# Later transposes of the expert lists in a two-layer decoder step

## The chip, the cores and the metric

The kernel runs on one core of a Trainium2 chip. The time is the device time of one execution in microseconds (us). Five engines work beside each other, each with a queue of its own that it takes strictly in order: TensorE (PE, and PEld for its weight loads), VectorE (DVE), ScalarE (ACT), GpSimd (POOL) and SyncE (SP, which only issues transfers here).

## The reference, cut to what matters

One inference step of a two-layer trunk (an RWKV-7 mixer, then a Mamba-2 mixer, each followed by an expert channel mixer called PEER) for a prompt of 256 tokens with 16 meta tokens, and for 32 sample tokens. The change lies in PEER, which runs once in each layer:

```python
q = (xt @ w_q).reshape(T, P_HEADS, 2, P_QDIM // 2)        # 8 heads, two half queries
s = jnp.einsum('thzd,zhkd->thzk', q, sub_keys)            # 128 scores a half
sv, si = lax.top_k(s, P_TOPK)                             # 16 best of each half
cand = sv[:, :, 0, :, None] + sv[:, :, 1, None, :]        # their 256 sums
top_s, pos = lax.top_k(cand..., P_TOPK)                   # 16 best of these: experts
gate = jax.nn.softmax(top_s, axis=-1)
act = jax.nn.gelu(jnp.einsum('td,ted->te', x_blk, u_tab[i_blk]))
out = jnp.einsum('te,ted->td', gate * act, v_tab[i_blk])  # 128 of 16384 experts a token
```

## The kernel before, in words

PEER (`peer`, line 838) does not gather the experts of the prompt tokens. It multiplies all 256 prompt tokens with the whole u table, in 128 blocks of 128 experts, takes GELU, multiplies the result by a sparse matrix of gates (zero for experts that a token has not chosen), and multiplies that with the whole v table in 128 blocks. Only the 48 sample and meta tokens (tile 0 of the selection) gather their expert rows by indirect transfers.

A **u product** (`s_chunk`, line 1060) is one such block: SP fetches 512 KB of weights (`wraw`, three buffers); ACT casts them to `whi` (line 276); POOL subtracts to get the low part `wlo` (line 281; `leng=LP` with LP = 8 gives POOL the whole of it in this stage); PE runs 16 matmuls with `whi` (lines 302 and 303) and 8 with `wlo` (line 305); ACT applies GELU from PSUM into `G` (line 1065). `whi` and `wlo` have two buffers each. The first 56 u products (b = 0 to 55, B0 = 56) run beside the selection.

The **expert selection** (`topk`, line 926 on) is nearly all DVE work: maxima, indices, candidate sums and a chain of comparisons (lines 957 to 1002) for three tiles: tile 0 (the sample and meta tokens, 64 rows), tiles 1 and 2 (two prompt tiles of 128 tokens). It is written as a generator of which the product loop takes a step or two a product, so its DVE work is interleaved with the products. They lie in a part of `G` that the one-hot stage fills later. Each tile ends with three lists on which the rest depends: `af` (line 1002) and `bf` (line 1001), the two halves of the expert numbers, and `ts`, the gates. For the gates three pieces are called later, from a table:

- `exps` (line 1004): ACT's exponential, which needs a table load before and another one behind it;
- `gates` (lines 1007 to 1009): DVE's sum, reciprocal and product, which give `ts`;
- `finish` (lines 1011 to 1017) for the prompt tiles: three PE transposes of `af`, `bf` and `ts` into one PSUM tile `ptk` (line 1014) and one ACT copy of it into `sel` (line 1017). For tile 0 the third piece is `indices` (lines 1019 on), which writes expert numbers through DRAM with POOL's transfers.

The table is `AFTER` (line 1075): row ti gives the u products behind which the three pieces of tile ti are called. Inside a PEER block a planner orders the instructions of each engine by its own estimate of time, but the first instruction of `exps` and `gates`, the first transpose and the copy are tied with `keep_in_program_order`: they stay behind everything of their engine that is written ahead of them.

Behind product 55 comes the **one-hot stage** (lines 1089 to 1124): for each group of four tokens DVE, ACT and POOL build two one-hot matrices from `sel` (`onehots`; three buffers, so three groups can be ready ahead), PE multiplies them (`pwt`, line 1120), DVE multiplies the result into `G` (line 1121) and ACT copies the rest (line 1122); ten more u products are mixed in. Tile 1's half of `sel` serves the first 32 groups, tile 2's half the last 32. Then come the v products (`acc`, line 1273) to the end of PEER.

Of the kernel before, what the change touches and what calls it, by code (L numbers as in the profile page):

```python
# [225 lines left out]
class K:  # L226
# [611 lines left out]
    def peer(self, l, ng):  # L838
# [233 lines left out]

        tk = chain(topk(0), topk(1), topk(2))

        AFTER = ((14, 16, 55), (29, 31, 39), (46, 46, 52))
        for b in range(B0):
            s_chunk(b, G[:, b], leng=LP if b < LB else None, tag="so"[b % 2])
            next(tk, None)
# [2 lines left out]
            for ti in range(3):  # L1081
                for i in range(3):
                    if b == AFTER[ti][i]:
                        late[ti][i]()
# [615 lines left out]
```

## Time and profile before

| | us |
|---|---|
| median of 3 runs (2675.41 to 2686.91) | 2676.23 |
| the profiled execution | 2676.22 |
| its span, first to last instruction | 2674.4 |

| engine | busy us | share of the span |
|---|---|---|
| PE | 2506.7 | 94% |
| PEld | 2156.3 | 81% |
| DVE | 1912.9 | 72% |
| ACT | 1246.7 | 47% |
| POOL | 1012.7 | 38% |

The profiled execution is 1.8 us longer than its span. PE is busy nearly all the time, so the question for each of its idle stretches is what ended it. Times in the rows count from the start of the span. The 56 products beside the selection stand near 500 to 690 us in the first layer and near 1820 to 2008 us in the second.

### The profile page before, as it was taken

The page shows a single profiled execution, that of the slowest core. Times are in us where ns is not written, and L with a number is a line of the kernel's source. Part 1 is how long each engine was busy: PE and PEld are TensorE (multiplying, and loading weights), DVE is VectorE, ACT ScalarE, POOL GpSimd, SP SyncE. Part 2 cuts the span into 40 slices and gives each one's busy share as a digit, 9 for nine tenths or more (in the row PEclk, how much of TensorE's full clock was granted, in tenths as well). Part 3 has the DMA queues.
Part 4 walks back from the last instruction along what each step waited for, and adds up shares of the span by engine and source line. Part 5 has one row for each costly group of instructions (what it writes and reads, how often), then busy time and mean ns, then how long its engine had stood idle before and what let it go on. Part 6 is the DMA issues. An engine that isn't in the chain of part 4 may idle for free. (4 is left out here: it accounts for less than half of the span.)

```text
span 2674.4 us, 47364 instructions
## 1 busy us (share of the span) xinstructions
PE 2506.7 (94%) x18281; PEld 2156.3 (81%) x18281; DVE 1912.9 (72%) x3713; ACT 1246.7 (47%) x2324; POOL 1012.7 (38%) x895
## 2 busy tenths in 40 slices
PE   7999999996989999999978888999979899999998
PEld 4677769996978888888765776899979788888886
DVE  5355556897695777788784787769949856776777
ACT  3322233453784444444454543335448744444444
POOL 4111110485980233424146455106959501122220
PEclk9999999998999999999999999999989999999999
DMA  3111115453417788888732443454633267788784
GB/s 148 52 46 44 41 58 174 138 179 105 136 42 213 255 304 303 299 301 311 256 93 87 146 154 124 129 181 148 184 110 114 62 217 250 259 279 260 262 270 156
DMA packets 125858, 460.68 MB, mean 172 GB/s; under 512 B 14816, under 2 KB 15744, under 8 KB 122432
## 3 DMA queue, kind: packets, MB, share of 16 engines
q1 hardware_dynamic: 99488, 361.08, 42.0%
q0 software_dynamic: 26144, 96.56, 10.1%
q8 instruction: 144, 2.36, 0.4%
q14 instruction: 82, 0.67, 0.1%
HBM read 440.90 MB, written 16.69 MB: 171 GB/s over the span
## 5 line engine op out<-in xcount | busy, mean ns | idle before, releaser
L276 ACT CAST whi<-wraw 128x1024 fp32r<-128x1024 f32 (+1 forms) x619 | 641.9, 1038 | 892.0 <-PE acc L1273 283.5
L283 DVE TENSOR_TENSOR wlo<-wraw,whi 128x1024 fp32r<-128x1024 f32 (+1 forms) x493 | 601.2, 1220 | 423.8 <-ACT whi L276 326.9
L302 PE MATMUL psc<-xh,whi 128*128 128x256 f32 x2048 | 509.0, 285 | 4.6 <-ACT h L1065 2.6
L303 PE MATMUL psc<-xl,whi 128*128 128x256 f32 x2048 | 507.0, 284 | 0.0
L281 POOL TENSOR_TENSOR wlo<-wraw,whi 128x1024 fp32r<-128x1024 f32 (+1 forms) x150 | 357.5, 2390 | 181.3 <-PE pq L305 72.5
L302 PEld LDWEIGHTS psc<-xh,whi 128*128 128x128 f32 x2048 | 392.8, 192 | 12.0 <-ACT whi L276 3.0
L303 PEld LDWEIGHTS psc<-xl,whi 128*128 128x128 f32 x2048 | 392.9, 192 | 5.6
L305 PE MATMUL psc<-xh,wlo 128*128 128x256 f32 x2048 | 291.6, 284 | 0.3 <-POOL wlo L281 0.3
L1051 POOL DMA_INDIRECT G<-in_un,gi x80 | 112.1, 1401 | 472.6 <-DVE glo L283 308.9
L1273 PE MATMUL acc<-whi,glo 128*128 128x512 f32 x1024 | 284.4, 398 | 6.7 <-DVE glo L283 6.7
L1273 PE MATMUL acc<-whi,gh 128*128 128x512 f32 x1024 | 284.6, 398 | 4.4 <-ACT whi L276 3.3
L1273 PE MATMUL acc<-wlo,gh 128*128 128x512 f32 x1024 | 281.8, 396 | 0.0
L305 PEld LDWEIGHTS psc<-xh,wlo 128*128 128x128 f32 x2048 | 265.2, 192 | 1.2 <-POOL wlo L281 0.7
L1273 PEld LDWEIGHTS acc<-whi,glo 128*128 128x128 f32 x1024 | 193.3, 189 | 54.6 <-DVE glo L283 7.6
L1148 POOL DMA_INDIRECT G<-in_v,gi x80 | 120.1, 1502 | 302.7 <-DVE G L1143 165.7
L1273 PEld LDWEIGHTS acc<-wlo,gh 128*128 128x128 f32 x1024 | 192.7, 189 | 47.8 <-DVE wlo L283 1.3
L1273 PEld LDWEIGHTS acc<-whi,gh 128*128 128x128 f32 x1024 | 184.0, 189 | 44.8 <-ACT whi L276 6.5
L1120 PE MATMUL pwt<-ob,oa 128*128 128x128 f32 x1024 | 144.7, 281 | 11.6 <-DVE ob L1094 8.0
L1120 PEld LDWEIGHTS pwt<-ob,oa 128*128 128x128 f32 x1024 | 127.7, 191 | 23.1 <-issue 19.2
L302 PE MATMUL pi<-xh,whi 128*128 128x320 f32 x328 | 107.0, 337 | 13.1 <-ACT cst L1369 4.7
L303 PE MATMUL pi<-xl,whi 128*128 128x320 f32 x328 | 105.8, 334 | 4.1 <-DVE xl L336 3.8
L283 DVE TENSOR_TENSOR glo<-G,gh 128x256 fp32r<-128x256 f32 x256 | 106.7, 418 | 2.7 <-ACT gh L276 2.7
(485 smaller groups left out, 4462.4 us busy)
## 6 DMA issues: line engine op xcount, KB each, us to landing
wraw<-in_u SPq DMA_DIRECT2D x256, 512.0 KB
wraw<-in_v SPq DMA_DIRECT2D x256, 512.0 KB
wraw<-in_win SPq DMA_DIRECT2D x41, 512.0 KB
wraw<-in_wq SPq DMA_DIRECT2D x32, 512.0 KB
wraw<-in_rkv SPq DMA_DIRECT2D x24, 512.0 KB
h<-in_ssm SPq DMA_DIRECT2D x8, 1024.0 KB
out_sssm<-h POOLq DMA_DIRECT2D x8, 1024.0 KB, 4.7
wraw<-in_wo SPq DMA_DIRECT2D x8, 512.0 KB
```

The costliest lines, as they stand in the source:

```text
L276: self.nc.scalar.copy(hi, x)
L281: self.nc.gpsimd.tensor_sub(lo[:, :n], x[:, :n], hi[:, :n].bitcast(F32))
L283: self.nc.vector.tensor_sub(lo[:, n:], x[:, n:], hi[:, n:].bitcast(F32))
L302: nc.tensor.matmul(ps, lhsT=whi[:, k], rhs=xhi[:, x0 + k], start=start and k == 0, stop=False)
L303: nc.tensor.matmul(ps, lhsT=whi[:, k], rhs=xlo[:, x0 + k], start=False, stop=False)
L305: nc.tensor.matmul(ps, lhsT=wlo[:, k], rhs=xhi[:, x0 + k], start=False, stop=stop and k == kb - 1)
L1051: nc.gpsimd.indirect_dma_start(out=rows, out_offset=None, in_=a[f"un{l}"], in_offset=bass.IndirectOffsetOnAxis(ap=gi[:, 0, g, m:m + 1], ax ...
L1120: mm(pw[:, j], lhsT=oa[:, j], rhs=ob[:, j], start=True, stop=True)
L1148: nc.gpsimd.indirect_dma_start(out=rows, out_offset=None, in_=vrows, in_offset=bass.IndirectOffsetOnAxis(ap=gi[:, 1, g, m:m + 1], axis=0))
L1273: mm(acc[i], lhsT=g[:, t0:t0 + 128], rhs=w[:, d0:d0 + 512], start=b == 0 and g is gh and w is vhf, stop=b == 127 and w is vlf)
```

## The change

The first prompt tile's transposes are called behind product 52 instead of 39, the second prompt tile's behind product 55 (the last of the 56) instead of 52. The second tile's `exps` and `gates` are called one product sooner, behind 45. Tile 0's row and tile 1's `exps` and `gates` stay.

```diff
-        AFTER = ((14, 16, 55), (29, 31, 39), (46, 46, 52))
+        AFTER = ((14, 16, 55), (29, 31, 52), (45, 45, 55))
         for b in range(B0):
             s_chunk(b, G[:, b], leng=LP if b < LB else None, tag="so"[b % 2])
             next(tk, None)
             if b % 2:
                 next(tk, None)
             for ti in range(3):
                 for i in range(3):
                     if b == AFTER[ti][i]:
                         late[ti][i]()
```

## Rows read from the trace of the kernel before

**Rows 1.** PE's waits, whole span: waiter, releaser, total us, times, longest.
```profile
PE ptk L1014 <- DVE G L1009: 20.5, 2, 10.2
PE ptk L1014 <- DVE G L1001: 18.7, 2, 9.4
```
**Rows 2.** PE in time, layer 0: start, us, line, operation, [idle before <-releaser].
```profile
614.22 1.12 PE L305 MATMUL psc<-xh,wlo 128*128 128x256 f32 x8
...
640.44 0.47 PE L1014 MATMUL ptk<-c,G 128*128 128x128 f32 x1 [10.23 <-DVE G L1009]
...
681.40 0.49 PE L1014 MATMUL ptk<-c,G 128*128 128x128 f32 x3
```
**Rows 3.** The same of layer 1.
```profile
1933.71 1.12 PE L305 MATMUL psc<-xh,wlo 128*128 128x256 f32 x8
...
1958.36 0.47 PE L1014 MATMUL ptk<-c,G 128*128 128x128 f32 x1 [10.23 <-DVE G L1009]
```
**Rows 4.** Stretches: length, busy PE, PEld, DVE, ACT, POOL (instructions), PE clock, DMA share, GB/s.
```profile
640.90:643.00 2.10, 2.10 (x12) 2.10 (x11) 2.07 (x2) 2.02 (x7) 1.45 (x3) 0.50 0.03 8
...
860.00:1200.00 340.00, 336.96 (x1919) 292.10 (x1918) 256.49 (x349) 158.85 (x238) 105.44 (x73) 1.00 0.85 290
```
**Rows 5.** PE in time, layer 0, products 13 and 14.
```profile
537.79 1.12 PE L305 MATMUL psc<-xh,wlo 128*128 128x256 f32 x8
540.67 1.12 PE L305 MATMUL psc<-xh,wlo 128*128 128x256 f32 x8
```
**Rows 6.** POOL in time, layer 0, before and behind the gap.
```profile
612.70 2.41 POOL L281 TENSOR_TENSOR wlo<-wraw,whi 128x1024 fp32r<-128x1024 f32 x1 [0.47 <-ACT whi L276]
...
641.55 0.81 POOL L1105 TENSOR_SCALAR oa<-cp,sel 128x128 f32<-128x128 f32 x1 [23.63 <-ACT sel L1017]
```
**Rows 7.** DVE in time, layer 0, inside PE's gap.
```profile
619.56 0.28 DVE L1002 TENSOR_TENSOR G<-G 128x128 f32<-128x128 f32 x1
...
622.31 2.27 DVE L996 TENSOR_TENSOR G<-G,cp 128x2048 bf16<-128x2048 f32 x1
...
625.95 0.27 DVE L984 TENSOR_TENSOR G<-G 128x128 f32<-128x128 f32 x1
...
632.79 1.22 DVE L992 TENSOR_TENSOR G<-G 128x1920 bf16<-128x1920 bf16 x1
...
640.10 0.28 DVE L1009 TENSOR_TENSOR G<-G 128x128 f32<-128x128 f32 x1
640.30 1.22 DVE L1000 TENSOR_TENSOR G<-G 128x2048 bf16<-128x2048 bf16 x1
641.55 2.29 DVE L1001 TENSOR_REDUCE G<-G 128x128 f32<-128x2048 bf16 x1
```
**Rows 8.** DVE in time, layer 0, ahead of the gap, beside POOL's subtractions.
```profile
556.59 2.71 DVE L989 TENSOR_TENSOR G<-G,cp 128x448 bf16<-128x448 bf16 x1
559.23 2.90 DVE L992 TENSOR_TENSOR G<-G 128x960 bf16<-128x960 bf16 x1
...
567.47 1.80 DVE L984 TENSOR_TENSOR G<-G 128x128 f32<-128x128 f32 x1
569.46 0.21 DVE L993 TENSOR_TENSOR G<-G 128x64 f32<-128x64 f32 x1
569.59 2.43 DVE L1002 TENSOR_TENSOR G<-G 128x64 f32<-128x64 f32 x1
...
584.72 3.21 DVE L996 TENSOR_TENSOR G<-G,cp 128x1024 bf16<-128x1024 f32 x1
```
**Rows 9.** DVE in time, layer 0, behind the gap.
```profile
643.76 0.76 DVE L1094 TENSOR_TENSOR ob<-cp,sel 128x512 f32<-128x512 f32 x1
...
648.49 2.42 DVE L1105 TENSOR_SCALAR oa<-cp,sel 128x128 f32<-128x128 f32 x1
...
668.40 1.46 DVE L1009 TENSOR_TENSOR G<-G 128x128 f32<-128x128 f32 x1
```
**Rows 10.** ACT in time, layer 0: the GELU of product 39.
```profile
615.41 0.38 ACT L1065 ACTIVATE G<-psc 128x256 f32<-128x256 f32 x1
```

## The prediction, on record before the changed kernel ran

> **What bounds the kernel now.** I read the busy shares first: PE is busy 94% of the span, so an idle stretch of PE is time lost unless something later absorbs it. Next the list of PE's waits over the whole span [rows 1]. Its two longest entries, 20.5 and 18.7 us, are the same instructions: the transposes `ptk` of a selection list, waiting for DVE. They come twice, once in each layer, so I read PE in order of time around the first of them [rows 2]. Product 39's last matmuls end at 614.22 + 1.12 = 615.34, then only three transposes run until 640.44 + 0.47 = 640.91. In the second layer the gap goes from 1934.83 to 1958.83 [rows 3]. In these gaps the other engines' rows say who works: POOL waits 23.63 us behind its last subtraction [rows 6], and DVE runs the tail of the selection without a pause [rows 7]. So for some 50 us in all this kernel is bound by DVE's list work and not by PE. The second tile's transposes, behind product 52, show no wait: three run in 0.49 us [rows 2].
>
> After the gap the work is PE's again: in the 340 us from 860 on PE is busy 336.96 [rows 4], so time saved ahead of that arrives at the end; I see no transfer or list that would hold it at an absolute time.
>
> **The change part by part.** The sum is made against the profiled execution's own 2676.22 us (span 2674.4 and 1.8 around it), which is the median, 2676.23, too.
>
> *The wait behind product 39 goes.* The gap is 640.91 - 615.34 = 25.6 us in layer 0 and 24.0 in layer 1. The three transposes themselves stay, 0.5 us without waits, so 25.1 and 23.5 go. Behind the gap PE runs 2.1 us at a granted clock of 0.50, the lower of its two levels (1.2 of 2.4 GHz), after it was idle [rows 4]; at full clock this work takes half, so another 1.05 us a layer. Together 26.1 + 24.5 = 50.6 us. That is the most the change can give.
>
> *What is late next.* Products 40 to 52 now follow at once. The pace is 2.88 us (537.79 to 540.67, [rows 5]); beside the selection it was 614.22 - 540.67 = 73.55 us for the 25 products 15 to 39, 2.94 each, so 13 products take 38.2 us with 0.8 of it lost to the neighbours. PE then reaches the first tile's transposes at 615.3 + 38.2 = 653.5 in layer 0 and 1973.0 in layer 1. The gates `ts` were ready at 640.10 + 0.28 = 640.4 [rows 7] and 1958.3 (the transposition that waited for them starts at 1958.36, [rows 3]). On those dates PE would not wait at all.
>
> But those dates were reached while POOL stood still. With no gap POOL subtracts on, 2.41 us of every 2.88 [rows 6], and DVE's instructions beside it are far longer. Compare the same lines without and with POOL: L1002 took 0.28 us in the gap and 2.43 ahead of it, on half the elements; L996 2.27 against 3.21 on half the elements (some 1.15 alone); L992 1.22 against 2.90 on half; L984 0.27 against 1.80; L989 took 2.71, on half the elements too, and L993 only 0.21 [rows 7, 8]. Some are stretched by about 2 us and some, which fall between two subtractions, not at all. From 618 us to the gates DVE has fifteen instructions of these kinds (tensor-tensor, scalar-tensor-tensor and cast): L993 twice, L1002 twice, L994 twice, L996 twice, and one each of L984, L1000, L982, L987, L989, L992 and L1009. By the rows: L1002 2 x 2.2 = 4.4, L996 2 x 2.1 = 4.2, L984 1.5, L992 2.90 - 0.61 = 2.3, L989 like L992 2.3, L1009 like L1002 2.2, L982 like L984 1.5, and nothing for L993, as its row shows, nor for L994, L987 and L1000, of which I have no stretched row. That is 18.4 us. Bounds: 0 if all find a gap, and 15 x 2.41 = 36 if each waits a whole subtraction. I take 18.4, since it goes line by line.
>
> The Trainium skill, page "SBUF — State Buffer", section "SBUF: two separate sides", says that DVE and GpSimd share a port pair under an exclusive lock which whoever starts first holds for its whole instruction. The stretched rows agree; read strictly, it would put the cost nearer to 36 us than to 18.4, which is the third case below.
>
> So `ts` of tile 1 is ready at 640.4 + 18.4 = 658.8 and 1958.3 + 18.4 = 1976.7. PE, there at 653.5 and 1973.0, waits 5.3 and 3.7 us. For a wait that short I take half of the 1.05 us of lower clock, 0.5 (ends 0 and 1.05).
>
> *The copy and the one-hots behind it.* ACT's copy into `sel` and POOL's first one-hot stand in their queues as before, now behind product 52. ACT holds the casts of the next weights meanwhile, but two are ready, and PE waits for the same event. What is new is the cover. DVE, ACT and POOL made the first three groups of one-hots 40 us ahead of their use. DVE spent 643.76 to 650.9 on them, 7.2 us [rows 9]. Now DVE, from 658.8 on, has L1000 and L1001 of tile 2 (1.22 + 2.29, [rows 7]), tile 2's gates (1.46 for the last of them, about 1.9 in all, [rows 9]) and then the one-hots: 658.8 + 3.5 + 1.9 + 7.2 = 671.4. PE, from 659 on, has three products (8.6 us) and the second transposes and is ready for `pwt` at 668.4. The first group is ready by then, the third is not. I charge 2 us a layer, between 0 and 3.0 (671.4 - 668.4).
>
> *The second tile.* Its transposes move behind product 55. PE gets there near 668 us, and `ts` of tile 2 is done near 664: no wait, 4 us of margin. Its `exps` (a table load, 0.31 us and a load back, as before) come one product sooner on ACT. ACT is there at the GELU of product 45: 615.41 + 0.38 + 6 x 2.9 = 633.2 [rows 10]. The maxima are subtracted (L984) at 626.2 in the gap [rows 7], and with L1002, L996 and L984 stretched (2.2 + 2.1 + 1.5) at 632.0: cost nothing, with 1 us of margin. POOL's index transfers of tile 0 stay behind product 55, SP's queue holds the same transfers in the same order, and both come sooner with PE. ACT's later copy over the lists follows `pwt`, which PE issues behind the transposes.
>
> *Sum.* Layer 0: 26.1 - 0.8 - 5.3 - 0.5 - 2.0 = 17.5. Layer 1: 24.5 - 0.8 - 3.7 - 0.5 - 2.0 = 17.5. 2676.2 - 35.0 = **2641 us**. Its own range, with half of the contention (9 us, no wait, nothing for the clock: gains of 23.3 and 21.7) and with half as much again (28 us: waits of 15 and 13, gains near 8): 2631 to 2660.
>
> **The rivals.**
> *All of it comes out.* If DVE's tail meets few subtractions and the one-hots hide under the last products, only 0 to 0.8 us a layer are lost: 2676.2 - 50.6 = 2625.6, or 2627. For it: DVE has 13 us of slack to the new place. Against it: five of the six lines in [rows 8] were stretched.
> *The wait only moves.* If all fifteen wait a whole subtraction (the strict reading of the skill's page), `ts` comes at 676.4 and PE waits 22.9 and 21.3 us at product 52. 26.1 - 22.9 - 0.8 - 1 = 1.4 and as much in layer 1: 2673. Against it: as soon as PE waits, POOL runs out of weights after two of them and DVE is free again, so it is more like 2660 at worst.
> *Slower.* ACT, tied behind product 45, takes `exps` of tile 2 in strict order. Should DVE's order or its contention bring L984 of tile 2 late, ACT waits with the casts behind it, and PE starves when the two buffered weights are used. Each us later than 633 + 5 costs PE one. The change is a loss when that exceeds 17.5 us a layer, L984 later than about 655. If the planner put L984 behind tile 1's gates (658.8) it would cost 21 a layer: 2676.2 + 2 x 3.5 = 2683. Against it: in the order of before L984 stands 14 us ahead of these gates.
> *Not what it says.* If the planner's other orders shift with the ties, so that PE waits elsewhere for the same lists, the time stays near 2676.
>
> **How the numbers follow.** Forecast 0.58; all of it 0.22; the wait moves 0.10; slower 0.04; nothing changes 0.06. The range 2623 to 2660 leaves out the last two and most of the third. A measurement can tell 0.5%, 13.4 us: faster means below 2662.8. That holds for the first two cases and half of the third, 0.85; within 0.5%: the other half and nothing changes, 0.11; slower than 2689.6 only if L984 is later still, 0.04.
>
> **What would show it.** PE's gap behind product 39 is gone, and a shorter one of some 4 to 5 us for L1009 stands ahead of the first `ptk` at about 654 us. DVE's L1002, L996, L992 and L1009 of tiles 1 and 2 are as long as ahead of the gap now. `pwt` begins 15 to 19 us sooner in each layer, and everything behind it keeps its length. Wrong would be: a wait of PE for `whi` near product 46 (ACT held by `exps`), a wait at product 52 above 12 us, or an unchanged DVE tail with a total near 2626.

## The result and the profile after

The changed kernel takes 2647.46 us (median of 4 runs, 2643.12 to 2648.49) against 2675.82 for the kernel before in the same comparison (4 runs, 2674.05 to 2686.91). The ratio is 0.9879, with a 95% interval of 0.9862 to 0.9895: 1.2% faster. In two later comparisons, on other runs, the changed kernel took 2641.48 us (ratio 0.9863, 0.9843 to 0.9882) and 2643.80 us (0.9875, 0.9858 to 0.9891). The forecast was 2641 us, a gain of 35.0 us; in the three comparisons the median lies 28.4, 35.2 and 34.1 us below that of the kernel before beside it. The profiled execution took 2643.12 us, with a span of 2641.3.

PE's waits over the whole span (waiter, releaser, total us, times, longest). In the kernel before there was a third one at `ptk`, beside the two of [rows 1]:

```profile
PE ptk L1014 <- DVE G L1002: 7.6, 2, 4.6
```

Of the changed kernel:

```profile
PE ptk L1014 <- DVE G L1009: 7.3, 2, 4.7
...
PE psc L305 <- POOL wlo L281: 1.6, 5, 0.5
...
PE pwt L1120 <- DVE ob L1103: 1.5, 1, 1.5
```

The waits for L1001 and L1002 are no longer in the list, and the one for L1009 has shrunk from 20.5 to 7.3 us. 20.5 + 18.7 + 7.6 = 46.8 us of waits at `ptk` have become 7.3. The two lowest lines are small: POOL's low parts were waited for once and for 0.3 us in the kernel before, and the one-hot of L1103 not at all.

PE in order of time, first layer 0 and then layer 1 (start, us, line, operation, [idle before <-releaser]); these lines answer to [rows 2] and [rows 3]:

```profile
655.17 1.12 PE L305 MATMUL psc<-xh,wlo 128*128 128x256 f32 x8
656.13 0.38 PE L1014 MATMUL ptk<-c,G 128*128 128x128 f32 x2
659.10 0.33 PE L1014 MATMUL ptk<-c,G 128*128 128x128 f32 x1 [2.59 <-DVE G L1009]
...
670.11 1.57 PE L1120 MATMUL pwt<-ob,oa 128*128 128x128 f32 x10 [1.53 <-DVE ob L1103]
...
674.28 0.49 PE L1014 MATMUL ptk<-c,G 128*128 128x128 f32 x3
```
```profile
1958.49 1.12 PE L305 MATMUL psc<-xh,wlo 128*128 128x256 f32 x8
1959.45 0.38 PE L1014 MATMUL ptk<-c,G 128*128 128x128 f32 x2
1964.58 0.48 PE L1014 MATMUL ptk<-c,G 128*128 128x128 f32 x1 [4.75 <-DVE G L1009]
```

Behind product 52 (the L305 line ahead of each) two transposes go at once, and the third waits for the gates. The three transposes of tile 2 (674.28) still wait for nothing. Stretches of the changed kernel (length, busy PE, PEld, DVE, ACT, POOL, PE clock, DMA share, GB/s), for [rows 4]:

```profile
653.90:660.10 6.20, 3.61 (x30) 3.38 (x30) 6.20 (x6) 3.02 (x6) 5.44 (x3) 1.00 0.46 124
660.10:663.60 3.50, 3.50 (x19) 3.50 (x18) 3.46 (x2) 3.50 (x11) 3.50 (x3) 0.51 0.69 213
860.00:1200.00 340.00, 335.57 (x1910) 290.38 (x1909) 259.28 (x353) 158.00 (x236) 110.97 (x76) 1.00 0.85 291
```

PE is busy for 3.61 of the 6.20 us around the wait, and in the 3.50 us behind it the granted clock is 0.51, the lower of its two levels. In the v products PE is busy 335.57 of 340 us, nearly as before.

Now the engines that set the date of the gates. DVE in order of time in layer 0, from 618 us to the gates; the lines answer to [rows 7], and they now look like those of [rows 8]:

```profile
618.69 1.57 DVE L993 TENSOR_TENSOR G<-G 128x128 f32<-128x128 f32 x1
620.18 0.28 DVE L1002 TENSOR_TENSOR G<-G 128x128 f32<-128x128 f32 x1
...
623.98 4.05 DVE L996 TENSOR_TENSOR G<-G,cp 128x2048 bf16<-128x2048 f32 x1
...
629.39 1.05 DVE L984 TENSOR_TENSOR G<-G 128x128 f32<-128x128 f32 x1
630.37 3.43 DVE L1000 TENSOR_TENSOR G<-G 128x2048 bf16<-128x2048 bf16 x1
633.72 2.43 DVE L982 CAST G<-G 128x128 f32<-128x128 uint32 x1
636.06 2.27 DVE L1001 TENSOR_REDUCE G<-G 128x128 f32<-128x2048 bf16 x1
638.26 2.18 DVE L987 TENSOR_TENSOR G<-G,cp 128x1920 bf16<-128x1920 f32 x1
640.47 3.17 DVE L989 TENSOR_TENSOR G<-G,cp 128x896 bf16<-128x896 bf16 x1
643.57 3.42 DVE L992 TENSOR_TENSOR G<-G 128x1920 bf16<-128x1920 bf16 x1
...
656.61 2.43 DVE L1009 TENSOR_TENSOR G<-G 128x128 f32<-128x128 f32 x1
```

POOL's subtractions in the same time, one line each:

```profile
626.35 3.94 POOL L281 TENSOR_TENSOR wlo<-wraw,whi 128x1024 fp32r<-128x1024 f32 x1 [0.48 <-ACT whi L276]
...
630.26 2.45 POOL L281 TENSOR_TENSOR wlo<-wraw,whi 128x1024 fp32r<-128x1024 f32 x1
...
632.68 3.38 POOL L281 TENSOR_TENSOR wlo<-wraw,whi 128x1024 fp32r<-128x1024 f32 x1
...
636.02 2.40 POOL L281 TENSOR_TENSOR wlo<-wraw,whi 128x1024 fp32r<-128x1024 f32 x1
...
638.38 4.31 POOL L281 TENSOR_TENSOR wlo<-wraw,whi 128x1024 fp32r<-128x1024 f32 x1
```

Read the two lists together. L996 stretches to 628.03; POOL's subtraction that started at 626.35 ends 2.26 us behind that, at 630.29, nearly its usual 2.41. L984, issued at 629.39, ends at 630.44, just behind that subtraction. POOL's next runs to 632.71, and L1000 ends 1.09 us later, against 1.22 alone [rows 7]. The next subtraction ends at 636.06, 2.26 us behind L1000, and the cast L982 ends at 636.15. So at these places the two engines take turns, and each instruction waits for the rest of the other's. Beside the reduction L1001 neither waits: it takes 2.27 us and the subtraction 2.40. L987 takes 2.18, as long as it does alone, because it starts 0.12 us ahead of a subtraction; that one pays instead, with 4.31.

The Trainium skill, page "SBUF — State Buffer", section "SBUF: two separate sides", says that the shared port pair goes to whoever starts first for its whole instruction and that the other blocks; the trace agrees, within some 0.15 us at each turn. The same page, section "Who interferes with whom", says that `tensor_reduce` never contends on this chip; L1001 and L998 (2.14 us with and without POOL) agree.

To compare kernels without what happens elsewhere I take the **stage** of a layer: from the GELU of product 39 to the last line of `pwt` in the one-hot stage. Before: 796.10 - 615.41 = 180.7 us in layer 0 and 2113.80 - 1934.90 = 178.9 in layer 1. The table has its gain in each traced kernel (us), layer 0 / layer 1. It also has the sum of the durations of the fifteen DVE instructions of the prediction, which was 12.65 and 13.84 us in the two gaps of the kernel before (tile 1's gates come last among them, so kernels with another order have none). The last column has what PE waited for up to its first one-hot product and with it, where a wait was 1 us or longer:

| kernel | stage gain | DVE's fifteen | PE's waits |
|---|---|---|---|
| changed | 19.2 / 17.3 | 31.97 / 34.33 | gates 2.6, one-hots 1.5 / gates 4.7 |
| changed, again | 19.3 / 16.6 | 31.96 / 34.18 | gates 2.6, one-hots 1.5 / gates 4.7 |
| changed, third | 17.9 / 19.5 | 32.09 / 30.22 | gates 5.6 / low parts 1.6 |
| no subtraction | 24.1 / 22.1 | 12.64 / 12.69 | none / none |
| first tile only | 14.9 / 11.5 | 31.95 / 32.93 | gates 2.6, L1001 5.2 / low parts 1.1, gates 2.8, L1001 5.2 |
| second tile only | -2.1 / -1.4 | 12.67 / 13.91 | L1002 4.6, L1001 9.5, gates 10.2 / L1002 3.0, L1001 9.5, gates 10.2 |
| second tie at 52 | 14.8 / 12.8 | 31.96 / 34.40 | gates 2.6, L1001 5.2 / gates 4.8, L1001 2.8 |
| first tie at 46 | 8.9 / 8.5 | 24.00 / 24.29 | gates 12.4 / gates 12.7 |
| early gates | 22.3 / 15.5 | - | none / one-hots 5.4 |
| early gates, again | 16.3 / 15.4 | - | one-hots 5.6 / one-hots 5.5 |
| gates 25, tie 50 | 20.1 / 17.8 | - | low parts 3.0, one-hots 1.2 / low parts 2.2, one-hots 2.6 |

### The profile page after: what moved, and what is told of

Same layout as the page of the kernel before. It is cut to its first block, busy times and chain, and to the rows that moved or that the text cites. A ratio compares the mean times of both kernels' runs of the same rounds, so it can differ in the third digit from the quotient of the medians.

```text
span 2641.3 us, 47368 instructions
## 1 busy us (share of the span) xinstructions
PE 2513.0 (95%) x18281; PEld 2160.8 (82%) x18281; DVE 1941.9 (74%) x3713; ACT 1246.8 (47%) x2324; POOL 1021.7 (39%) x895
## 3 DMA queue, kind: packets, MB, share of 16 engines
q0 software_dynamic: 26144, 96.56, 10.2%
## 5 line engine op out<-in xcount | busy, mean ns | idle before, releaser
L281 POOL TENSOR_TENSOR wlo<-wraw,whi 128x1024 fp32r<-128x1024 f32 (+1 forms) x150 | 371.0, 2483 | 175.6 <-PE pq L305 72.5
L305 PE MATMUL psc<-xh,wlo 128*128 128x256 f32 x2048 | 292.9, 285 | 1.8 <-POOL wlo L281 1.6
L305 PEld LDWEIGHTS psc<-xh,wlo 128*128 128x128 f32 x2048 | 265.8, 192 | 3.9 <-POOL wlo L281 3.4
```

The source lines that it names most:

```text
L281: self.nc.gpsimd.tensor_sub(lo[:, :n], x[:, :n], hi[:, :n].bitcast(F32))
L305: nc.tensor.matmul(ps, lhsT=wlo[:, k], rhs=xhi[:, x0 + k], start=False, stop=stop and k == kb - 1)
```

## The experiments

Each row of `AFTER` gives the products behind which `exps`, `gates` and the transposes of one tile are called. Every experiment starts from the changed kernel; where only the new line is shown, it replaces the changed kernel's.

### Which half of the change does it

Only the first prompt tile's transposes move; the second tile keeps its row of before:

```diff
-        AFTER = ((14, 16, 55), (29, 31, 52), (45, 45, 55))
+        AFTER = ((14, 16, 55), (29, 31, 52), (46, 46, 52))
```

> Only the first tile's tie is moved (39 to 52); the second tile keeps 52, with its exponentials and gates behind 46. Theory (the time is what DVE's list work leaves open between products): behind product 52 PE now needs both tiles' gates. The first are ready near 659 us, the second only some 5 us later, so PE waits about 5 us more in each layer than in the changed kernel, and has products 53 to 55 still to do: 2653 to 2660, most of the gain kept. Rival (the move of the second tie is worth nothing): 2647 with a single wait of under 5 us.

2647.46 us (4 runs, 2647.07 to 2650.61), ratio 0.9887 (0.9869 to 0.9904). Behind product 52 PE now waits twice, for tile 1's gates (2.6 and 2.8 us) and for tile 2's list from L1001 (5.2 in each layer). The stage gains 14.9 and 11.5 us: most of the change, not all of it. The time lies below the expected 2653 to 2660 and on the rival's 2647, but the rival's single wait is not what the trace shows.

Only the second tile's row is the new one, and the first keeps 39:

```diff
+        AFTER = ((14, 16, 55), (29, 31, 39), (45, 45, 55))
```

> Only the second tile's ties are moved (transposes behind 55, exponentials and gates behind 45); the first tile's transposes stay behind 39. Theory: the gap of 24 to 25 us behind product 39 is there in both layers, and the second tile's transposes had no wait to lose: 2672 to 2680. Rival (the order of the one-hot stage, not the gap, gave the gain): 2660 or less.

2678.27 us (10 runs, 2674.55 to 2682.57), ratio 0.9997 (0.9987 to 1.0006): nothing, as expected. While PE stands behind product 39 no transposition of the second tile waits, so there is nothing for its tie to save. The gain comes from the gap behind product 39; the second tie matters only once that is gone.

### Is DVE's stretch POOL's work

In the changed kernel products 40 to 52 take the high part of their weights as the low part too, so their subtraction on POOL is left out (and their low-part products are other numbers); PE's, ACT's and DVE's work stays:

```diff
-            w = self.load_w(a[f"u{l}"][b], heng=heng, leng=leng)
+            if 40 <= b <= 52:
+                raw = self.fetch(a[f"u{l}"][b])
+                hi = self.wp.tile([128, 8, 128], F32R, name="whi", tag="whi")
+                nc.scalar.copy(hi, raw)
+                w = (hi, hi)
+            else:
+                w = self.load_w(a[f"u{l}"][b], heng=heng, leng=leng)
```

> The changed kernel, but for products 40 to 52 POOL's subtraction is left out (the high part of the weights is used in place of the low part, so PE does the same matmuls). Theory (DVE's list tail is stretched by POOL's subtractions): L1002, L992, L996, L982 and L1009 take again what they took in the old gap (0.28, 1.22, 2.27, 0.21, 0.28 us), the first tile's gates are ready near 642 us instead of 659, PE does not wait at product 52, 2634 to 2641. Rival (they are stretched by something else that now runs, ACT's casts, PE's reads or the transfers): the lengths stay above 2 us, the wait of 3 to 5 us stays, 2645 to 2648.

2629.55 us (4 runs, 2624.66 to 2633.86), ratio 0.9816 (0.9795 to 0.9837), below the expected 2634 to 2641. POOL in layer 0, its first subtraction behind product 39, and then DVE, the same instructions as above:

```profile
652.02 2.40 POOL L281 TENSOR_TENSOR wlo<-wraw,whi 128x1024 fp32r<-128x1024 f32 x1 [39.55 <-ACT whi L276]
```
```profile
618.50 2.27 DVE L996 TENSOR_TENSOR G<-G,cp 128x2048 bf16<-128x2048 f32 x1
...
622.14 0.27 DVE L984 TENSOR_TENSOR G<-G 128x128 f32<-128x128 f32 x1
622.33 1.21 DVE L1000 TENSOR_TENSOR G<-G 128x2048 bf16<-128x2048 bf16 x1
623.47 0.21 DVE L982 CAST G<-G 128x128 f32<-128x128 uint32 x1
...
627.98 1.09 DVE L989 TENSOR_TENSOR G<-G,cp 128x896 bf16<-128x896 bf16 x1
628.99 1.22 DVE L992 TENSOR_TENSOR G<-G 128x1920 bf16<-128x1920 bf16 x1
...
636.30 0.28 DVE L1009 TENSOR_TENSOR G<-G 128x128 f32<-128x128 f32 x1
```

With POOL idle for 39.55 us every line is back at its length in the gap [rows 7], though PE multiplies on, ACT casts on and the weights still come: 12.64 and 12.69 us for the fifteen. The gates are ready at 636.58, sooner than the expected 642, and no transposition waits. So the stretch comes from POOL's subtractions, and the rival (casts, PE's reads or the transfers) is out. This is the prediction's "all of it comes out" made real: stage gains of 24.1 and 22.1 against the 26.1 and 24.5 worked out as the most that there is. POOL's work costs the changed kernel 4.9 us of stage in layer 0 and 4.8 in layer 1 (24.1 - 19.2 and 22.1 - 17.3).

### Where the first tie belongs

The first tile's transposes at product 46, six products earlier than in the change:

```diff
+        AFTER = ((14, 16, 55), (29, 31, 46), (45, 45, 55))
```

> The changed kernel with the first tile's transposes behind product 46 instead of 52. PE comes there near 637 us. Theory (the gates' date depends on POOL: when PE waits POOL soon stops, and DVE's tail runs free): the gates come near 651 us instead of 659, PE waits about 14 us, but only some 4 us a layer are lost against the changed kernel: 2650 to 2657. Rival (the gates come at 659 whatever POOL does): a wait of 20 us, 16 a layer lost: above 2672.

2660.84 us (6 runs, 2657.21 to 2662.70), ratio 0.9935 (0.9920 to 0.9949): 19.4 us above the changed kernel's 2641.48 in the same comparison. Both expectations missed; "only 4 us a layer" was a slip, since the wait that it gave, 14 us against 4, is 10 more. The gate's transposition and then DVE, in layer 0:

```profile
653.59 0.48 PE L1014 MATMUL ptk<-c,G 128*128 128x128 f32 x1 [12.40 <-DVE G L1009]
```
```profile
642.90 3.11 DVE L989 TENSOR_TENSOR G<-G,cp 128x896 bf16<-128x896 bf16 x1
645.94 1.21 DVE L992 TENSOR_TENSOR G<-G 128x1920 bf16<-128x1920 bf16 x1
...
653.25 0.28 DVE L1009 TENSOR_TENSOR G<-G 128x128 f32<-128x128 f32 x1
```

While PE waits, POOL runs out of weights to subtract (it is idle from 645.07 on, for 9.63 us), and from 645.94 on DVE's instructions have their short lengths: a wait partly pays for itself, as the prediction said of its second rival. The fifteen take 24.0 us instead of 32.0. Even so PE has lost 12.4 us instead of 2.6.

The tie a little earlier than in the change, at 50, with both tiles' gates sooner:

```diff
+        AFTER = ((14, 16, 55), (25, 25, 50), (44, 44, 55))
```

> First tile: exponentials and gates behind product 25, transposes behind 50; second tile: exponentials and gates behind 44, transposes behind 55. DVE's order then has L1009 of the first tile right behind L987, so its gates are ready near 643 us and no wait is left even at product 50 (649 us); the first one-hots are made two products sooner. Theory: as with gates behind 27 (2639) or 1 to 4 us better: 2634 to 2639. Rival (POOL's one-hots push its subtractions back, and PE waits for these instead): 2639 to 2646.

2639.59 us (4 runs, 2637.19 to 2640.72), ratio 0.9855 (0.9836 to 0.9873); its median is 1.9 us below the changed kernel's 2641.48, and the two intervals overlap widely. No transposition waits, but PE waits for low parts instead, as the rival said: POOL's first four one-hots, from 655.51 to 661.30, stand ahead of the subtraction. PE's waits from 640 to 690 us:

```profile
PE psc L305 <- POOL wlo L281: 3.6, 2, 3.0
PE pwt L1120 <- DVE ob L1103: 1.2, 1, 1.2
```

### What the second tie is worth

The second tile's transposes at product 52 instead of 55, everything else as in the change:

```diff
+        AFTER = ((14, 16, 55), (29, 31, 52), (45, 45, 52))
```

> The changed kernel with the second tile's transposes behind product 52 instead of 55 (exponentials and gates stay behind 45). In the run with 52 and 46 the trace had 5 us more of waits a layer, but the time was that of the changed kernel. Theory A (the wait is real and lost; that run's remainder was scatter): 2652 to 2657. Theory B (it is given back: while PE waits POOL is idle and DVE gets on, and what PE then does is work that fits later): 2645 to 2649.

2647.99 us (4 runs, 2643.70 to 2651.36), ratio 0.9886 (0.9866 to 0.9906), against 2641.48 (0.9863, 0.9843 to 0.9882) for the changed kernel beside it. The intervals overlap, and the time lies in theory B's range. But that range was set against 2647 for the changed kernel; against the 2641.48 beside it, 6.5 us are lost, as theory A had it (5 to 10). The traces show where. PE in layer 0:

```profile
653.98 0.38 PE L1014 MATMUL ptk<-c,G 128*128 128x128 f32 x2
656.95 0.44 PE L1014 MATMUL ptk<-c,G 128*128 128x128 f32 x2 [2.59 <-DVE G L1009]
662.56 0.47 PE L1014 MATMUL ptk<-c,G 128*128 128x128 f32 x1 [5.17 <-DVE G L1001]
```

The second tile's lists come later too, now that POOL goes on. The stages gain 14.8 and 12.8 us, against 19.3 and 16.6 in the changed kernel's trace of the same comparison: the move from 52 to 55 is worth 4.5 and 3.9 us. It is the same wait that the first experiment showed.

The changed kernel ran beside these three:

> The changed kernel once more, as the measure for the three beside it: its first four times were 2643 to 2648, and the profiled one was the fastest of them. 2644 to 2649 expected by every theory.

2641.48 us (4 runs, 2637.95 to 2643.92), below the 2644 to 2649 that every theory expected. Its waits are those of the first trace, 2.6 and 4.7 us for the gates and 1.5 for a one-hot.

### Can the rest of the wait be had

The first tile's `exps` three products sooner and its `gates` four, so that DVE does L1009 among the lists and not at their end:

```diff
+        AFTER = ((14, 16, 55), (26, 27, 52), (45, 45, 55))
```

> The changed kernel with the first tile's exponentials and gates called behind products 26 and 27 instead of 29 and 31, so that DVE's last list instruction of that tile (L1009) stands ahead of four others. Theory (what is left of the wait is DVE's order and its stretched tail): the first gates are ready near 652 us, before PE comes at 655; the waits of 4.7 and 2.6 us at product 52 go, and with them a piece of lower clock: 2636 to 2641. Rival (the wait goes over to the next list, the second tile's at product 55 or the one-hots): 2644 to 2648.

2638.83 us (5 runs, 2632.76 to 2641.98), ratio 0.9845 (0.9828 to 0.9863): what the theory expected, with no changed kernel beside it.

> The first tile's exponentials and gates behind products 26 and 27, on one chip with the changed kernel. The waits it removes are 2.6 and 4.7 us, with some lower clock: 4 to 9 us under the changed kernel beside it. Rival (what is left goes into POOL's one-hots and the scatter): within 3 us of it.

The same kernel again: 2643.61 us (4 runs, 2638.34 to 2644.53), ratio 0.9866 (0.9850 to 0.9883). Beside it the changed kernel:

> The changed kernel, measured beside it: 2639 to 2649, as its two medians so far (2647.5 and 2641.5).

2643.80 us (4 runs, 2639.15 to 2646.12), ratio 0.9875 (0.9858 to 0.9891). The first run of the early gates looked like a gain of 3 to 9 us over the changed kernel; side by side the medians differ by 0.2, as the rival said. PE's waits of the early gates, in the second comparison, from 640 to 690 us:

```profile
PE pwt L1120 <- DVE ob L1103: 5.6, 1, 5.6
```

The wait has gone from `ptk` to the first one-hots, which DVE makes behind the same lists. So it is in three of the four stages of the two traces (5.4, 5.6 and 5.5 us): DVE's work as a whole is late at this place, and the tie moves only the point at which PE meets it. In the fourth, layer 0 of the first trace, there is no such wait, and the stage gained 22.3 us.

## Why the prediction was right, step by step

*The most that the change can give, 26.1 + 24.5 us.* Right as a bound: with POOL out of the way the stage gains 24.1 + 22.1.

*Pace of the 13 products.* Forecast 38.2 us with 0.8 lost. From the low-part matmuls of product 39 (they start at 616.34 and 1919.46) to those of product 52 (655.17 and 1958.49) they took 38.8 and 39.0 us, so 1.4 and 1.6 were lost to the pace of 2.88. PE waited for low parts in both (idle for 0.5 and 0.8 us), since POOL's subtractions are lengthened in their turn: the nine from 626.35 on took 27.66 us, 3.07 each. This effect of the turns on POOL was not in the sum.

*DVE's stretch, 18.4 us.* Measured as 31.97 - 12.65 = 19.3 us in layer 0 and 34.33 - 13.84 = 20.5 in layer 1 (there the first L993 still took 1.50 us in the gap, beside the last subtraction). The mechanism was right, and that the total came so close is partly luck, since lines missed both ways: L1000 was costed at nothing, having no stretched row, and takes 2.2 us more; L993 also at nothing, and takes 1.3 and 1.5 more; one L994 takes 1.0 more. Against that one L1002 and one L996 found a free moment. The gates were forecast at 658.8 in layer 0, and are ready at 656.61 + 2.43 = 659.04. In layer 1, on the dates of the kernel before, the forecast was 1976.7; the layer's first GELU comes 14.25 us sooner in the changed kernel, which makes it 1962.5, and they are ready at 1964.53.

*PE's wait at product 52, 5.3 and 3.7 us.* Measured 2.6 and 4.7. To leave out that this execution came 2.1 us late into layer 0 (product 39's low parts at 616.34 instead of 614.22 [rows 2]), count from product 39's GELU. In layer 0 the gates were forecast 658.8 - 615.4 = 43.4 us behind it and came 659.04 - 617.54 = 41.5 behind it, and PE came 39.0 behind it (656.51) instead of 38.1, 0.9 later: 5.3 - 1.9 - 0.9 = 2.5. The gates came sooner although the stretch was longer, because DVE began the fifteen 1.15 us behind that GELU, and in the kernel before 619.37 - 615.41 = 3.96 behind it:

```profile
617.54 0.38 ACT L1065 ACTIVATE G<-psc 128x256 f32<-128x256 f32 x1
```

(The first of the fifteen is the L993 at 618.69, shown above.) The prediction kept the start of the list as it read it in one execution, without a reason; the last section shows that this start changes from execution to execution. In layer 1 DVE began 1.16 us behind the GELU in both kernels. There the gates came 2.1 later than forecast, through the longer stretch, and PE 1.1 later: 3.7 + 2.1 - 1.1 = 4.7.

*The lower clock, 0.5 us a layer.* Too small: 3.5 us at a granted clock of 0.51 cost about 1.7 us behind the wait of layer 0. In layer 1 the clock fell while PE still waited and was back at 1967.4, after 2.8 us of work, which makes 1.4. Even the wait of 2.6 us was followed by it. In the kernel before, the lower clock lasted to 643.7, 2.80 us and not the 2.1 that the sum took, so 0.35 us a layer more came back there.

*The one-hots, 2.0 us a layer between 0 and 3.0.* Measured 1.5 in layer 0 and no wait in layer 1.

*The second tile, nothing.* No wait, as forecast; its transposes came at 674.28, its gates at 665.15 + 2.42 = 667.57. But the prediction named only the margin and not what the tie's old place would have cost. Without that move the stages would gain some 8 us less in all (4.5 + 3.9 in the experiment on the second tie). Its `exps` cost nothing: L984 ended at 630.44 and the exponential ran at 636.72, behind its table load, so that the slower rival did not start. POOL, behind ACT's casts, was not idle from 626.35 to 654.01.

*The sum.* Layer 0: 26.1 + 0.35 - 1.4 - 2.6 - 1.7 - 1.5 = 19.2, and the stage gained 19.2. Layer 1: 24.5 + 0.35 - 1.6 - 4.7 - 1.4 = 17.2, and it gained 17.3. Forecast were 17.5 and 17.5. In layer 0 the pace and the clock, forecast too small, cost 1.8 us more, and the gates and the one-hots 3.2 less; so the agreement of the total owes something to errors that cancel. The forecast of 35.0 in all stands against 36.5, 36.0 and 37.4 in the three traces of the changed kernel. The end moved by 33.1 us in the first of them, because 3.4 us went elsewhere: 2.1 early in the run, 1.9 in the v products of layer 0, 1.0 between the layers, and 1.5 came back in layer 1.

*The signs.* PE's gap behind product 39 is gone, and a shorter wait for L1009 stands behind product 52, ahead of the third transposition and not of the first. DVE's stretched lines are there. One sign was wrong: `pwt` was to begin 15 to 19 us sooner, with everything behind it as long as before. In layer 0 it begins at 670.11 instead of 681.73, which is 13.8 sooner counted from product 39's GELU, and 11.6 sooner in layer 1. The other 5.5 and 5.7 us of the stage's gain lie between the first and the last `pwt`: the kernel before began `pwt` behind product 52, with products 53 to 55 still to come among the one-hots (low parts at 683.51, 686.39 and 689.45), and the changed kernel has only the end of product 55 there (673.32).

*The rivals.* All of it comes out: only without the subtractions. The wait moves: its premise, a whole subtraction for each of the fifteen, is wrong. In the rows above the turn does pass only at the end of an instruction; but a DVE instruction arrives somewhere inside a subtraction and waits for its rest, four of the fifteen (L1002, L987, L994 and L996, once each) found no subtraction running or only the end of one, and in between stand reductions and index instructions, which took no longer beside a subtraction (L1001 2.27 us, the indices 0.20 each). That makes 1.3 us each (19.3 / 15), not 2.41.

## What to carry to other kernels

When a wait of the main engine is removed, cost the late list anew: the others had the chip to themselves while the main engine stood, and their durations in the gap are not those that they will have. Take the stretched lengths from a place where all engines run, or look for the two instructions that exclude each other and count the turns. And when a tie moves the place of a wait, sum the waits of the whole stage and not that of one instruction, since the next consumer of the same engine may inherit it.

## What was not expected of the hardware

The same program, with the same order of instructions, meets POOL at another moment in different executions. In layer 1, DVE of the first trace of the changed kernel, and then of the third:

```profile
1955.20 2.37 DVE L1002 TENSOR_TENSOR G<-G 128x128 f32<-128x128 f32 x1
...
1957.82 4.37 DVE L996 TENSOR_TENSOR G<-G,cp 128x2048 bf16<-128x2048 f32 x1
1962.11 2.42 DVE L1009 TENSOR_TENSOR G<-G 128x128 f32<-128x128 f32 x1
```
```profile
1953.16 0.28 DVE L1002 TENSOR_TENSOR G<-G 128x128 f32<-128x128 f32 x1
...
1953.67 2.29 DVE L996 TENSOR_TENSOR G<-G,cp 128x2048 bf16<-128x2048 f32 x1
1955.88 2.44 DVE L1009 TENSOR_TENSOR G<-G 128x128 f32<-128x128 f32 x1
```

In the third trace the second L1002 found no subtraction, and L996 did not have to wait for one. The gates were ready at 1958.32 instead of 1964.53; 2.1 of these 6.2 us are an earlier start of the stage, 4.1 the two instructions. No transposition waited, and PE waited 1.6 us for a low part instead.

In layer 0 the third trace went the other way, with a wait of 5.6 us for the gates. There a single instruction of tile 0, some 55 us earlier, tells the two kinds of execution apart. L992 of tile 0 in the first trace:

```profile
561.36 0.68 DVE L992 TENSOR_TENSOR G<-G 128x960 bf16<-128x960 bf16 x1
```

In the third it took 2.89 us, and its GELU of product 39 and first L993 were:

```profile
615.60 0.38 ACT L1065 ACTIVATE G<-psc 128x256 f32<-128x256 f32 x1
619.63 1.57 DVE L993 TENSOR_TENSOR G<-G 128x128 f32<-128x128 f32 x1
```

In the first trace POOL's next subtraction started at 561.73, just behind L992; in the kernel before it started at 559.08, 0.15 us ahead of L992, which took 2.90 [rows 8]. In the eleven traces that keep the subtractions, L992 took 0.68 in six, and there DVE began the fifteen 1.15 us behind product 39's GELU; it took 2.9 in the other five, the kernel before among them, and there DVE began 3.96 to 4.03 behind it. So a few tenths of a us near 560 go with some 2.9 us, about one product, near 618. That is how the traces go together; no run forced it. The second trace, whose stage began at 615.48 as that of the kernel before did, had the 0.68, the 1.15 and a wait of 2.6.

Some 4 us of the scatter between runs of the changed kernel (2638 to 2648) may come from this: its stages gained 17.9 to 19.3 us in layer 0 and 16.6 to 19.5 in layer 1. That is an inference from three traces. For the same reason the small differences between the changed kernel, the early gates and the tie at 50 stay undecided.
